# Three of eight up projections as seven products, and short products ahead of the down projections

## The chip, the cores and the metric

The kernel runs on one core of a Trainium2 chip. The metric is device time in microseconds (us). The kernel before takes 867.45 us (median of 3 runs, 867.34 to 867.73). A separate, profiled execution gave the page and the trace; the profile's rows are read from that one execution.

## What the kernel computes

One decoder layer on 512 tokens of width 1024, all in float32:

```python
h = rmsnorm(x)
q, k, v, xr, gr, g_attn, g_rnn = split(h @ w_in)          # seven blocks of 1024 columns
A = differential attention(q, k, v)                        # 8 heads, QK-norm, relative bias, causal
R = gelu(gr) * rg_lru(causal_conv4(xr))
x = x + (sigmoid(g_attn) * (A @ w_proj_attn) + sigmoid(g_rnn) * (R @ w_proj_rnn)) @ w_out
h2 = rmsnorm(x)
x = x + square(relu(h2 @ w_up)) @ w_down                   # 1024 -> 4096 -> 1024
```

The change touches the last two lines above all, and what runs beside the recurrent branch R.

## The kernel before

**Split float32.** A product of float32 operands is made of three passes in a rounded format. Each operand is split into a high part (a cast, on ACT) and a rest (source minus high part, a subtraction on DVE). `mm3` adds high x high, high x rest and rest x high into one accumulator. So every weight tile of 128 x 1024 (512 KB) costs one load, one cast on ACT and one subtraction on DVE: `wraw` or `raw` is the loaded tile, `whi` the cast and `wlo` the rest. There are five pairs of `whi` and `wlo` in the MLP, so weights are prepared up to four ahead, and four buffers for loads (`wraw` x2, `rx` x2).

**Stages.** Tokens lie along the columns of the moving operand. In order: the projections of `w_in` (q, k and v with attention mixed in, lines 136 to 138, products of 256 columns with `hT` as the stationary operand), the gates and the recurrent branch (products of 512 columns), the merge with `w_proj_*`, then `w_out` (`merged`), then the MLP. V tiles (`v`) and probability tiles (`pt`) are the operands of attention times V.

**Weights up to `w_out`.** Two objects of the class `Weights`, `wa` and `wb`, hold two streams of weight tiles that share two load buffers. In the recurrent part each has one load outstanding (`raws` = 1): the next load starts when the rest of the tile before it has been made. `wb` brings the 16 tiles of the recurrent branch's own projections.

**The MLP** is written out as a list of `steps`. The width of 4096 is cut into eight up groups of 512 columns, and the down projection into four pairs: pair d reads up groups 2d and 2d+1 and makes both halves of the output, (d, 0) and (d, 1). The order before is: up 0, 1, 2, down pair 0, up 3, 4, down pair 1, up 5, 6, down pair 2, up 7, down pair 3.

**Plain up group:** 8 blocks of the width 1024, 4 blocks of 128 output columns, 3 passes: 96 matmuls of 512 columns. Its result goes through relu and square on ACT (`up_out`) into `q`.

**Down product:** each (d, m) is a 2 x 2 block product done as seven products (Strassen's scheme in Winograd's form, named M1 to M7) in place of eight. One product has 2 x 4 x 3 = 24 matmuls of 256 columns, so (d, m) has 168. For it the activations are kept in seven forms: the four blocks and three more made of their sums and differences (`fs`; there are four sums, `FORM` says which form a product reads). The weights are summed as well: M5 takes b0 + b1, M6 takes b0 + b1 + b3, M7 takes b1 + b3, M4 takes b2 plus the sum. These sums are made in SBUF, by DVE (`plus`) and by accumulating transfers of POOL's queue. An output is added up by DVE (`down_out`) as soon as its product is done.

**Order of the work.** ACT, DVE and POOL run in the order in which the program is written (`InOrder`). `ahead` casts the next weights after each step. `later(us, f)` puts a piece of work some us of PE time later in that order; `tick` moves this clock on.

Of the kernel before, what the change touches and what calls it, by code (L numbers as in the profile page):

```python
# [37 lines left out]
def tile_block(ctx: ExitStack, tc: tile.TileContext, x, w_in, w_rga, w_rgx, w_pa, w_pr, w_o,  # L38
# [7 lines left out]
    sm = ctx.enter_context(tc.tile_pool(name="sm", bufs=4))  # L46
    es_ps = ExitStack()
# [169 lines left out]
    hT = hp.tile([P, 2 * KT * S + 64], F32R, tag="hT", name="hT")  # L217
    hT = [hT[:, 16 + j * KT * S:16 + (j + 1) * KT * S].rearrange("p (k s) -> p k s", k=KT) for j in range(2)]
# [38 lines left out]
    for j in range(4):  # L257
        wb.cols(w_o, 256 * j)
# [119 lines left out]
    wk = es_at.enter_context(tc.tile_pool(name="wk", bufs=1, reuse_waits="tile"))  # L378
    toep = [wk.tile([P, S], F32, tag=f"toep{h}", name=f"toep{h}") for h in range(NH)]
# [37 lines left out]
    def lam_diff(lt):  # L417
        lv = lt[:, :256].rearrange("p (a b c) -> p a b c", a=2, b=2)
        pv = lt[:, 256:384].rearrange("p (a c) -> p a c", a=2)
        V.tensor_tensor(out=pv, in0=lv[:, :, 0, :], in1=lv[:, :, 1, :], op=ALU.mult)  # L420
        t2 = lambda n: sm.tile([P, 2], F32, name=n, tag=n, bufs=1)
        ls, le = t2("ls"), t2("le")
        V.tensor_reduce(out=ls, in_=pv, axis=AX.X, op=ALU.add)
        A.activation(le, ls, AF.Exp)
        V.scalar_tensor_tensor(out=lneg, in0=le[:, 1:2], scalar=-LAMBDA_INIT, in1=le[:, 0:1], op0=ALU.add, op1=ALU.subtract)

    def softplus():
        lam = smt[:, C_LM:C_LM + KT]
        t8 = lambda n: sm.tile([P, KT], F32, name=n, tag=n, bufs=1)
        ab, e, den, s, s2, po, tmp, mx = (t8(n) for n in ("ab", "e", "den", "s", "s2", "po", "tmp", "mxl"))  # L430
# [391 lines left out]
    with tc.tile_pool(name="rp", bufs=1, reuse_waits="tile") as rp:  # L822
        fill = chain(ga, y_attn())
        side = []

# [40 lines left out]
        mh = hp.tile([P, 2, KT, S], F32R, tag="hT", name="mT")  # L866
        mh = [mh[:, j] for j in range(2)]
# [6 lines left out]
    h2T = [fin.tile([P, KT, S], F32R, tag=f"h2T{j}", name=f"h2T{j}") for j in range(2)]  # L874
# [3 lines left out]
    onesr = fin.tile([P, P], F32R, name="onesr")  # L878
    r2 = fin.tile([P, S], F32, name="r2")
    scratch = fin.tile([P, 4, S], F32, tag="us1", name="scratch")  # L880
    V.memset(scratch[:, 0, :P], 1.0)
    V.tensor_copy(onesr, scratch[:, 0, :P])
    ssq = scratch[:, 1, :]
    owing = []

    def merged(j):
        def done(ps):
            for c in range(2):
                t = 2 * j + c
                V.tensor_tensor(out=x2[:, t, :], in0=ps[c], in1=x2[:, t, :], op=ALU.add)  # L890
                split(h2T[0][:, t, :], h2T[1][:, t, :], x2[:, t, :], smt[:, C_G2 + t:C_G2 + t + 1])
            for c in range(2):
                t = 2 * j + c
                sq = ssq if t == 0 else scratch[:, 2 + t % 2, :]
                A.activation(sq, x2[:, t, :], AF.Square)
                if t:
                    owing.append(lambda sq=sq: V.tensor_tensor(out=ssq, in0=ssq, in1=sq, op=ALU.add))
# [6 lines left out]
    for d, ups in enumerate(((0, 1, 2), (3, 4), (5, 6), (7,))):  # L904
        steps += [("up", 2 * n + i // 2, i % 2, None) for n in ups for i in range(4)]
        if d < 3:
            steps += [("dn", (d, m), p, every) for m in range(2) for p in ORDER7]
        else:
            g, r = range(3), range(3, 4)
            steps += [("dn", (d, 0), p, q) for q in (g, r) for p in ("M1", "M2", "M5")]  # L910
            steps += [("dn", (d, 0), p, every) for p in ("M6", "M7", "M3", "M4")]
            steps += [("dn", (d, 1), p, every) for p in ORDER7]
# [4 lines left out]
    for kind, a, p in ops:  # L917
        if kind == "up":
            loads.append(((kind, a, p), w_up[p, a]))
        else:  # L920
            b = w_dn[2 * a[0] + a[1]].rearrange("a b p c -> (a b) p c")
            for q in (0, 1, 3, 2):
# [22 lines left out]
    def can_cast():  # L945
# [5 lines left out]
        return all((kind, a, q) in raw for q in ((p,) if kind == "up" else uses[p]))  # L951
# [14 lines left out]
    def cast_hi():  # L966
# [4 lines left out]
        src = raw[kind, a, p if kind == "up" else uses[p][0]]  # L971
        own = n % 5 == 4
        hi, lo = weight_pair(0 if own else 64, fin if own else None)
# [4 lines left out]
    def cast_lo():  # L978
# [3 lines left out]
        if kind == "up":  # L982
# [10 lines left out]
        if not half:  # L993
            plus(len(units))
# [28 lines left out]
    forms = [None] * 8  # L1023

    def hi_part(dst, src):
        A.copy(dst[:, 0], src)

    def lo_part(dst, src):
        V.tensor_tensor(out=dst[:, 1], in0=src, in1=dst[:, 0].bitcast(F32), op=ALU.subtract)

    def up_out(a, ps):
        n = a // 2
        if a % 2 == 0:
            t = hp.tile([P, 7168], F32R, tag="hT", name="us") if n % 3 == 0 else fin.tile([P, 7168 + 64], F32R, tag=f"us{n % 3}", name="us")
            t = t if n % 3 == 0 else t[:, 48:48 + 7168]
            forms[n] = t.rearrange("p (r f h s) -> p r f h s", r=2, f=7, h=2)
        d = forms[n][:, :, :, a % 2, :]
        q = fin.tile([P, 2, 2, 256], F32, tag="q", name="q")
        fs = fin.tile([P, 4, 256], F32, tag="fs", name="fs")
        w = 0.0 if a == 15 else 1.0  # L1040
        for c in range(2):
            A.activation(q[:, c, ::-1, :], two(ps[c]), AF.Relu)
            A.activation(q[:, c], q[:, c], AF.Square)
        a11, a21, a22, a12 = q[:, 0, 1], q[:, 0, 0], q[:, 1, 0], q[:, 1, 1]

        def sums():
            for m, (x, y, op) in enumerate(((a21, a22, ALU.subtract), (fs[:, 0], a11, ALU.subtract), (a11, a21, ALU.subtract), (a12, fs[:, 1], ALU.add))):
                V.tensor_tensor(out=fs[:, m], in0=x, in1=y, op=op)

        def first_hi():  # L1050
            hi_part(d[:, :, 0], a11)
            hi_part(d[:, :, 1:3], q[:, 1])

        def first_lo():
            lo_part(d[:, :, 0], a11)
            lo_part(d[:, :, 1:3], q[:, 1])

        later(w * 1.0, first_hi)
        if w == 0:
            later(0.0, first_lo)  # L1060
        later(w * 2.5, sums)
        later(w * 3.5, lambda: hi_part(d[:, :, 3:7], fs))
        if w:
            later(3.6, first_lo)
        later(w * 5.0, lambda: lo_part(d[:, :, 3:7], fs))
# [18 lines left out]

    def norm2():
        s2 = fin.tile([P, 2, S], F32R, tag="us2", name="s2")
        split(s2[:, 0], s2[:, 1], ssq)
        ps = psum("acc")
        T.matmul(ps, onesr, s2[:, 0], start=True, stop=False)
        T.matmul(ps, onesr, s2[:, 1], start=False, stop=True)  # L1090
        V.tensor_scalar(out=r2, in0=ps, scalar1=1.0 / DM, scalar2=EPS, op0=ALU.mult, op1=ALU.add)
        for t in range(KT):
            later(2.0 + 2.5 * t, lambda t=t: V.tensor_tensor(out=x2[:, t, :], in0=x2[:, t, :], in1=r2, op=ALU.mult))
        later(32.0, lambda: V.reciprocal(r2, r2))

    for j in range(4):
        if j == 2:
            wb.raws = 2
        for n, _ in enumerate(merged(j)):
            load()  # L1100
            while owing and n == 1:
                owing.pop(0)()
            if j == 3 and len(wb.units) == len(wb.reqs):
                ahead()
    while owing:
        owing.pop(0)()
    slots[0] += 1
    seen, banks, ps = {}, {}, None
    for n, (kind, a, p, pairs) in enumerate(steps):
        o = kind, a, p  # L1110
        if kind == "dn" and a not in banks:
# [93 lines left out]
```

## Time and profile before

| | |
|---|---|
| median of 3 runs | 867.45 us |
| profiled execution | 867.03 us |
| its span, first to last instruction | 865.3 us |
| PE busy | 859.6 us, 5239 matmuls |
| DVE, ACT, POOL busy | 602.1, 427.1, 64.3 us |
| DMA | 99.28 MB |
| granted TensorE clock | 1.00 |

PE is TensorE's matmul row and PEld its weight loads, which overlap with it. DVE is VectorE, ACT ScalarE, POOL GpSimd, SP the engine that issues most loads. Rows of groups read "line engine operation out<-in shapes xcount | busy us, mean ns | idle time before". Matmuls are pipelined: a 256-column one lasts about 0.28 us, but the next starts after 0.11 to 0.12, so a pace is taken from starts and not from lengths. Stages in the trace: projections and attention up to about 287 us, recurrent part and merge 287 to 486, `w_out` 486 to 529, MLP from 529. Line 66 is the helper that issues everything on ACT, DVE and POOL.

### The profile page before, as it was taken

What the parts mean: (1) busy time and instruction counts of PE and PEld (TensorE: products, weight loads), DVE (VectorE), ACT (ScalarE), POOL (GpSimd) and SP (SyncE); (2) the same over time, 40 slices, a digit from 0 to 9 for tenths busy, and PEclk for the clock granted to TensorE, in tenths of its full rate; (3) what the DMA queues carried; (4) which work ended last, traced back from release to release, by engine and by line L of the source; (5) the groups of instructions that cost most, each with busy time, mean ns of one, the idle gap of its engine ahead of it and who ended that gap; (6) DMA issues with size and microseconds to landing.
All of it is one profiled execution on the core that took longest, in us unless ns stands there. A gap on an engine that the chain in (4) does not pass through costs nothing.

```text
span 865.3 us, 13211 instructions
## 1 busy us (share of the span) xinstructions
PE 859.6 (99%) x5239; PEld 756.8 (87%) x5239; DVE 602.1 (70%) x1052; ACT 427.1 (49%) x679; POOL 64.3 (7%) x71
## 2 busy tenths in 40 slices
PE   9999999999999999999999999999999999999998
PEld 7899999999888888888888888889988998899898
DVE  6765688887866345978876656777746775667577
ACT  7444356464545337577653335556345444544341
POOL 0031212213011100000000000000000000000000
PEclk9999999999999999999999999999999999999999
DMA  6358212221321443323213723223652364246354
GB/s 199 120 167 242 93 57 81 64 84 63 108 64 42 114 137 98 110 86 97 73 55 123 259 99 129 92 89 81 168 173 73 103 173 140 72 128 189 87 134 122
DMA packets 33118, 99.28 MB, mean 115 GB/s; under 512 B 3984, under 2 KB 8792, under 8 KB 33056
## 3 DMA queue, kind: packets, MB, share of 16 engines
q1 hardware_dynamic: 29856, 87.93, 31.2%
q0 software_dynamic: 3200, 10.50, 6.4%
q8 instruction: 41, 0.67, 0.3%
q14 instruction: 21, 0.17, 0.1%
HBM read 87.89 MB, written 4.76 MB: 107 GB/s over the span
## 4 chain that ended last, share of the span: by engine, by line
PE 93%; DVE 4%; ACT 2%; DMA 1%; issue 1%; SPq 0%
PE acc L136 22%; PE acc L137 22%; PE acc L138 22%; PE acc L1154 18%; PE at L532 2%; PE at L137 2%; PE at L136 2%; PE at L138 2%; PE at L566 1%; DVE wlo L66 1%; DVE pe L66 1%; PE at L484 1%; PE at L597 1%; ACT pe L66 1%; DMA xT<-in_x_dram 1%
## 5 line engine op out<-in xcount | busy, mean ns | idle before, releaser
L1154 PE MATMUL acc<-us,whi 128*128 128x256 f32 x896 | 157.7, 280 | 0.0
L66 DVE TENSOR_TENSOR wlo<-wraw,whi 128x1024 fp32r<-128x1024 f32 (+2 forms) x86 | 96.8, 1147 | 72.6 <-ACT whi L66 72.2
L66 ACT CAST whi<-raw 128x1024 fp32r<-128x1024 f32 x88 | 90.6, 1049 | 102.0 <-DVE raw L66 41.6
L1154 PEld LDWEIGHTS acc<-us,whi 128*128 128x128 f32 x896 | 136.8, 188 | 0.4
L1154 PE MATMUL acc<-us,wlo 128*128 128x256 f32 x448 | 125.5, 280 | 0.0
L66 DVE TENSOR_TENSOR wlo<-raw,whi 128x1024 fp32r<-128x1024 f32 x88 | 106.5, 1217 | 16.1 <-ACT whi L66 15.8
L136 PE MATMUL acc<-whi,hT 128*128 128x256 f32 x384 | 109.7, 286 | 0.0
L137 PE MATMUL acc<-wlo,hT 128*128 128x256 f32 x384 | 107.2, 279 | 0.2 <-DVE wlo L66 0.2
L138 PE MATMUL acc<-whi,hT 128*128 128x256 f32 x384 | 107.0, 279 | 0.0
L66 ACT CAST whi<-wraw 128x1024 fp32r<-128x1024 f32 (+2 forms) x86 | 82.5, 981 | 42.7 <-DMA wraw<-in_w_in_dram 29.0
L138 PE MATMUL acc<-h2T,wlo 128*128 128x512 f32 x256 | 99.6, 389 | 0.0
L136 PE MATMUL acc<-h2T,whi 128*128 128x512 f32 x256 | 99.6, 389 | 0.0
L137 PE MATMUL acc<-h2T,whi 128*128 128x512 f32 x256 | 99.6, 389 | 0.0
L1154 PEld LDWEIGHTS acc<-us,wlo 128*128 128x128 f32 x448 | 85.7, 191 | 0.0
L136 PE MATMUL acc<-hT,whi 128*128 128x512 f32 x208 | 82.2, 395 | 0.0
L137 PE MATMUL acc<-hT,whi 128*128 128x512 f32 x208 | 81.2, 390 | 0.0
L138 PE MATMUL acc<-hT,wlo 128*128 128x512 f32 x208 | 81.0, 389 | 0.0
L136 PEld LDWEIGHTS acc<-whi,hT 128*128 128x128 f32 x384 | 72.3, 188 | 4.3 <-issue 3.0
L137 PEld LDWEIGHTS acc<-wlo,hT 128*128 128x128 f32 x384 | 72.2, 188 | 1.0 <-issue 0.5
L138 PEld LDWEIGHTS acc<-whi,hT 128*128 128x128 f32 x384 | 72.2, 188 | 0.6 <-issue 0.4
L66 ACT ACTIVATE pe<-pe,nm 128x128 f32<-128x128 f32 (+3 forms) x64 | 35.5, 556 | 66.0 <-DVE nm L66 66.0
L66 DVE TENSOR_TENSOR x<-acc,x 128x512 f32<-128x512 f32 (+1 forms) x52 | 33.2, 646 | 40.4 <-PE acc L1154 31.0
(192 smaller groups left out, 1605.9 us busy)
## 6 DMA issues: line engine op xcount, KB each, us to landing
wraw<-in_w_in_dram SPq DMA_DIRECT2D x54, 512.0 KB, 3.5
raw<-in_w_up_dram SPq DMA_DIRECT2D x32, 512.0 KB, 4.4
raw<-in_w_dn_dram SPq DMA_DIRECT2D x32, 512.0 KB, 3.5
raw<-raw POOLq DMA_DIRECT2D x16, 512.0 KB, 4.6
wraw<-in_w_pa_dram SPq DMA_DIRECT2D x8, 512.0 KB, 4.2
wraw<-in_w_pr_dram SPq DMA_DIRECT2D x8, 512.0 KB, 3.4
wraw<-in_w_o_dram SPq DMA_DIRECT2D x8, 512.0 KB, 3.5
trep<-tdram SPq DMA_DIRECT2D x8, 320.0 KB, 4.8
```

What stands on the lines that cost most here:

```text
L66: ins = f(*a, **k)
L136: T.matmul(o, l[0], r[0], start=first, stop=False)
L137: T.matmul(o, l[0], r[1], start=False, stop=False)
L138: T.matmul(o, l[1], r[0], start=False, stop=last)
L484: T.transpose(out=ps[:, t * P:(t + 1) * P], in_=qn[t // 2][:, c0:c0 + P], identity=ident)
L532: T.matmul(lg[c][:, :N], qT[r, x0, i * P:(i + 1) * P], kT[r, y0, :N], start=a == 0, stop=a == 2)
L566: T.transpose(out=tp[:, b * P:(b + 1) * P], in_=st[s][:, b * P:(b + 1) * P], identity=ident)
L597: T.matmul(ps[:, t:t + 1], sq[:, t * P:(t + 1) * P], ones, start=True, stop=True)
L1154: T.matmul(d, l[:, i, P * u:P * u + P], act[:, r, f, i % 2], start=p in ("M1", "M2", "M5") and k == z == e == 0 and (u == 0 or isinstance( ...
```

## The change

Up groups 2, 4 and 6 are done as seven products like the down projection; the other five stay plain. The order becomes, for d = 0 to 3: up 2d, up 2d+1, down pair d. For the seven products the moving operand `h2` holds the four blocks of each pair of width blocks and their four sums (made in `merged` for all), and the outputs are put together by `up_out` from the accumulators: M1 is copied out, M2 added, M5, M7, M6 and M3 combined, then relu and square. The summed weights (M5, M6, M7, M4 of three groups) are made by `weight_sums` with 30 transfers on POOL's queue, called at the head of the recurrent part: a tile is loaded, others are added to it on the way by accumulating loads, and each sum is stored in DRAM. There the groups load them like any weight.

A first product of 64 columns is put ahead of M1 of each (d, 0): it uses M1's first weights, and M1 starts its accumulator anew over it, so nothing of it stays ("empty"). `hT` and `mT` are cut into 14 slices and 2 (`Halves`; the last two live in the tile `tail`, which later holds sums). Ten small tiles move from the pool `sm` to the head of the attention pool, and fillers (`apart`, `apart2`) are added, so that V, the probability tiles and what follows stand at other addresses. Shifts of weight tiles change (`w_o` 64 bytes, plain up groups 0 or 192 in place of 64 or 0). The matmuls of the MLP are issued in written order too. The three-quarter first products of the last pair go.

```diff
+    stg = es_act.enter_context(tc.tile_pool(name="stg", bufs=1, side="right"))
+    summed = [{p: dp.tile([P, 1024], F32, name=f"up{n}{p}") for p in ("M5", "M7", "M6", "M4")} for n in range(2, 8, 2)]
+    def weight_sums():
+        t = stg.tile([P, 1024], F32, name="sum")
+        for n in range(2, 8, 2):
+            for blocks in (((0, None), (1, "M5"), (3, "M6"), (2, "M4")), ((1, None), (3, "M7"))):
+                for b, p in blocks:
+                    if p:
+                        G.dma_start(t, w_up[n, b], accum_op=ALU.add)
+                        G.dma_start(summed[n // 2 - 1][p], t)
+                    else:
+                        G.dma_start(t, w_up[n, b])
...
     wk = es_at.enter_context(tc.tile_pool(name="wk", bufs=1, reuse_waits="tile"))
+    t2 = {n: wk.tile([P, 2], F32, name=n) for n in ("ls", "le")}
+    t8 = [wk.tile([P, KT], F32, name=n) for n in ("ab", "e", "den", "s", "s2", "po", "tmp", "mxl")]
+    wk.tile([P, 32], F32, name="apart2")
...
         side = []
+        weight_sums()
...
-                split(h2T[0][:, t, :], h2T[1][:, t, :], x2[:, t, :], smt[:, C_G2 + t:C_G2 + t + 1])
+                A.activation(q[:, 2 * c:2 * c + 2], x2[:, t, :].rearrange("p (u s) -> p u s", u=2), AF.Copy, scale=smt[:, C_G2 + t:C_G2 + t + 1])
+            for c in range(2):
+                hi_part(d[:, :, 2 * c:2 * c + 2], q[:, 2 * c:2 * c + 2])
+                lo_part(d[:, :, 2 * c:2 * c + 2], q[:, 2 * c:2 * c + 2])
+            def sums():
+                fs = fin.tile([P, 4, 256], F32, tag="fs", name="fs")
+                sums_to(fs, *(q[:, m] for m in (1, 0, 3, 2)))
+                hi_part(d[:, :, 4:8], fs)
+                late.append(lambda: lo_part(d[:, :, 4:8], fs))
...
+    for d in range(4):
+        if d:
+            products("up", 2 * d)
         else:
+            products("pl", 0, ("b0", "b2", "b1", "b3"))
+        products("pl", 2 * d + 1, ("b0", "b2", "b1", "b3"))
+        products("dn", (d, 0))
+        products("dn", (d, 1))
...
+    def up_out(n, p, X, Y, Z):
+        if p == "M1":
+            begin(n)
+            snap = fin.tile([P, 2, 256], F32, tag="fs", name="snap")
+            A.copy(snap, two(Y))
+            quads[n] = fin.tile([P, 4, 2, 256], F32, tag="q", name="q"), snap
+            return
+        q, snap = quads[n]
+        if p == "M5":
+            A.copy(q[:, 2], two(Z))
+        elif p == "M6":
+            A.copy(q[:, 3], two(Y))
+        elif p == "M2":
+            V.tensor_tensor(out=q[:, 1], in0=two(X), in1=snap, op=ALU.add)
+            later(1.0, lambda: squared(q, 1, 2))
...
+        elif p == "M7":
+            V.tensor_tensor(out=q[:, 2], in0=q[:, 2], in1=two(Y), op=ALU.subtract)
+        elif p == "M3":
+            V.tensor_tensor(out=q[:, 3], in0=two(Z), in1=q[:, 3], op=ALU.subtract)
+            later(1.0, lambda: squared(q, 2, 4))
...
+        elif p == "M4":
+            squared(q, 0, 1, two(Y))
+            fs = rests()
+            later(2.0, lambda: total(n, fs, 0, 1))
+            later(4.9, lambda: total(n, fs, 2, 3))
...
+    def plain_out(n, c, u, ps):
...
+        A.activation(q[:, 2 * c:2 * c + 2][:, ::-1, u], two(ps), AF.Relu)
+        A.activation(q[:, 2 * c:2 * c + 2, u], q[:, 2 * c:2 * c + 2, u], AF.Square)
...
+        for m in range(2):
+            total(n, fs, m, u=u)
+            part(n, hi_part, 3 + m, 4 + m, fs[0][:, m:m + 1, u], u)()
+        for m in range(2):
+            part(n, lo_part, 3 + m, 4 + m, fs[0][:, m:m + 1, u], u)()
...
+        if kind == "dn" and a[1] == 0 and p == "M1" and k == 0:
+            I.matmul((b[0] if isinstance(b, tuple) else b)[:, :64], hi[:, 0, :P], forms[2 * a[0]][:, 0, f, 0, :64], start=True, stop=True)
         for u in range(2):
             d = b[u][:, :256] if isinstance(b, tuple) else b[:, 256 * u:256 * u + 256]
             for z, i in enumerate(pairs):
                 for e, (l, r) in enumerate(((hi, 0), (hi, 1), (lo, 0))):
-                    T.matmul(d, l[:, i, P * u:P * u + P], act[:, r, f, i % 2],
+                    act = h2[:, r, i, ACT8[p]] if kind == "up" else forms[2 * a[0] + i // 2][:, r, f, i % 2]
+                    I.matmul(d, l[:, i, P * u:P * u + P], act, start=p in ("M1", "M2", "M5") and k == z == e == 0 and (u == 0 or isinstance(b, tuple)),
```

More of the change, by code (lines that the diff above doesn't have):

```diff
@@ L46, in tile_block @@
     sm = ctx.enter_context(tc.tile_pool(name="sm", bufs=4))
+    sm.tile([P, 16], F32, name="apart", bufs=1)
     es_ps = ExitStack()
@@ L865, in tile_block @@
         wb.ahead, wb.raws = 3, 2
-        mh = hp.tile([P, 2, KT, S], F32R, tag="hT", name="mT")
-        mh = [mh[:, j] for j in range(2)]
+        mh = Halves("mT", 16)
         run(y_rnn(mh))
@@ L950, in can_cast @@
         kind, a, p = ops[n]
-        return all((kind, a, q) in raw for q in ((p,) if kind == "up" else uses[p]))
+        return all((kind, a, q) in raw for q in (uses[p] if kind == "dn" else (p,)))
     added, cast = set(), set()
@@ L992, in cast_lo @@
             G.dma_start(raw[kind, a, "b1"], raw[kind, a, "b3"], accum_op=ALU.add)
-        if not half:
+        if not half and more:
             plus(len(units))
@@ L1022, in tile_block @@
     two = lambda b: b.rearrange("p (u s) -> p u s", u=2)
[L1023 to L1065, printed above, removed]
@@ new lines, in total, with rests @@
+    def total(n, fs, *ms, u=slice(0, 2)):
+        q = quads[n][0][:, :, u]
+        fs = [f[:, :, u] for f in fs]
+        for m in ms:
+            x, y, op = ((q[:, 0], q[:, 2], ALU.subtract), (fs[0][:, 0], q[:, 1], ALU.subtract), (q[:, 1], q[:, 0], ALU.subtract), (q[:, 3], fs[0][:, 1], ALU.add))[m]
+            V.tensor_tensor(out=fs[m // 2][:, m % 2], in0=x, in1=y, op=op)
+    def rests():
+        return hp.tile([P, 2, 2, 256], F32, tag="tail", name="fs"), fin.tile([P, 2, 2, 256], F32, tag="fs", name="fs")
```

229 lines of the change are left out of this document (155 added, 74 removed).

## The prediction

> **What bounds the kernel now.** I read the page first (busy shares, the chain of waits), then the chain by stretches, then the TensorE rows whose first and last start give a pace, then the rows of the weight path (DMA, cast, rest) where PE comes nearest to waiting.
>
> ```profile
> span 865.3 us, 13211 instructions
> PE 859.6 (99%) x5239; PEld 756.8 (87%) x5239; DVE 602.1 (70%) x1052; ACT 427.1 (49%) x679; POOL 64.3 (7%) x71
> ...
> PE 93%; DVE 4%; ACT 2%; DMA 1%; issue 1%; SPq 0%
> ```
>
> The chain that ended last runs 93% through PE, at full granted clock. So the sum is one of matmul counts times paces, plus whatever new waits the change makes. The paces, from the view of one tile (plain up stage, products of 512 columns), from the chain (down stage, products of 256; columns: start, length, what; the first pair, the last one, its end) and from the groups of the page:
>
> ```profile
> L138 PE MATMUL acc<-h2T,wlo x69: 389/389/393, 548.7 to 595.0; 128*128 128x512 f32 x69
> 595.38 39.57 PE acc L1154 x336
> 822.90 38.83 PE acc L1154 x336
> 836.90 24.83 PE acc L1154 x219
> L1154 PE MATMUL acc<-us,whi 128*128 128x256 f32 x896 | 157.7, 280 | 0.0
> ```
>
> In the up stage every third matmul is one of these 69, so a 512-column matmul takes (595.0 - 548.7) / (68 x 3) = 0.2270 us. A 256-column one takes 39.57 / 336 = 0.1178 us in the first of the four down pairs, and the two in the middle are as long ((157.7 - 38.83) / 3 = 39.6); but in the end of the last pair it takes 24.83 / 219 = 0.1134 us. These are two paces of the same products, 0.0044 us apart. I call them slow and fast. Where they change (timeline of PE: start, length, what; a row may hold several):
>
> ```profile
> 190.12 0.28 PE L138 MATMUL acc<-whi,hT 128*128 128x256 f32 x1
> 190.82 0.28 PE L138 MATMUL acc<-whi,hT 128*128 128x256 f32 x1
> ...
> 222.91 0.60 PE L484 MATMUL at<-ident,qn 128*128 128x128 f32 x4
> 223.26 0.37 PE L136 MATMUL acc<-whi,hT 128*128 128x256 f32 x1
> 223.47 0.28 PE L137 MATMUL acc<-wlo,hT 128*128 128x256 f32 x1
> 223.58 0.28 PE L138 MATMUL acc<-whi,hT 128*128 128x256 f32 x1
> ...
> 834.28 0.36 PE L1154 MATMUL acc<-us,wlo 128*128 128x256 f32 x1
> 834.48 0.40 PE L1154 MATMUL acc<-us,whi 128*128 128x256 f32 x2
> ```
>
> At 834.28 one product starts 0.20 us before the next instead of 0.12, and from 836.90 at the latest the pace is the fast one and stays so. At 222.91 four short transposes come between; the stream after them settles at 0.113 too. At 190.12, a few matmuls behind another batch of short ones, the pace is 0.117 (six starts in 0.70 us): that one settled slow. So a hiccup of PE can switch the pace, in most cases to fast. A stream that follows 512-column products without one is slow from its first matmul: all four down pairs start that way.
>
> **The change part by part.** The sum is made against the profiled execution (865.3 us, 867.0 with what lies around it); the median shown is 867.45, 0.4 above, and I carry differences over to that.
>
> *Up groups 2, 4, 6 as seven products.* Each loses 96 matmuls of 512 columns and gains 7 x 24 = 168 of 256. Removed: 288 x 0.2270 = 65.4 us. Added: 504 x 0.1134 = 57.1 at the fast pace, 504 x 0.1178 = 59.4 at the slow one. Term: **-8.2** (slow: -6.0). By the rows a 256-column product costs half a 512-column one. The Trainium skill (TensorE: Matmul & The Clock Gate, Back-to-back issue gap) says otherwise: sustained 131 ns for 512 columns and 81 for 128. An estimate on a straight line gives 98 for 256, and by it three groups would cost 3 x (168 x 98 - 96 x 131) ns = 11.7 us more instead. This case's 227 and 113 to 118 ns disagree, and the measurement decides.
>
> *Empty products at the head of four down pairs.* Each is one 64-column matmul with the first weights between the 512-column stream and the down products; this is the place where slow begins now. If it acts like the short matmuls at 222.91, all 1344 down products and the seven-product group that follows each pair run fast. The four pairs take 3 x 39.57 + 38.83 = 157.5; 1344 x 0.1134 = 152.4. Term: **-5.2** (slow throughout: +0.8, since the last pair loses its fast part). One empty product costs between 0.11 (one weight load, as two fast products are apart) and 0.25 (a break such as 223.26 to 223.47, with settling): four cost **+0.6**.
>
> *V elsewhere.* Ten small tiles move from one pool to the head of the attention pool, so V and the probability tiles get other addresses.
>
> ```profile
> L138 PE MATMUL at<-pt,v x48: 276/281/283, 103.9 to 283.5; 128*128 128x256 f32 x48
> L136 PE MATMUL acc<-whi,hT x384: 276/276/390, 41.2 to 225.7; 128*128 128x256 f32 x192
> L1154 PE MATMUL acc<-us,whi x145: 276/276/276, 836.9 to 861.3; 128*128 128x256 f32 x145
> ```
>
> The triples are shortest, median and longest in ns. A fast product lasts 276 (last row), so attention-times-V is mostly slow (median 281) and the projections, which come after breaks as well, are mostly fast. 144 products, between 144 x 0.0044 = -0.6 and 0; I take **-0.3**. The same for hT, whose last two slices move: nothing, with the same kind of unknown.
>
> *Sums of weights in the recurrent part.* 30 transfers of 512 KB on POOL's queue, one after the other through one staging tile (6 loads, 12 accumulating loads, 12 stores). Between this row and its first add of the down stage POOL has nothing,
>
> ```profile
> 291.07 0.54 POOL L66 DMA_DIRECT2D rb<-rdram  x1 [1.71 <-ACT gate L66]
> wraw<-in_w_in_dram SPq DMA_DIRECT2D x54, 512.0 KB, 3.5
> raw<-in_w_up_dram SPq DMA_DIRECT2D x32, 512.0 KB, 4.4
> raw<-raw POOLq DMA_DIRECT2D x16, 512.0 KB, 4.6
> ```
>
> so they start at 292 and, at 4.6 us and an issue each, need some 150 to 165 us, until 450; the first down pair comes at 573, their first reader after 600. They are not late themselves, but they run beside the weight loads of the recurrent part, of which one is outstanding at a time there, exactly where PE has no reserve (ACT's casts with what they waited for, then the rests on DVE, then PE's first use of a rest):
>
> ```profile
> 305.31 2.00 ACT L66 CAST whi<-wraw 128x1024 fp32r<-128x1024 f32 x2 [3.02 <-DMA wraw<-in_w_in_dram]
> 311.29 1.05 ACT L66 CAST whi<-wraw 128x1024 fp32r<-128x1024 f32 x1 [3.98 <-DMA wraw<-in_w_in_dram]
> ...
> 306.40 2.36 DVE L66 TENSOR_TENSOR wlo<-wraw,whi 128x1024 fp32r<-128x1024 f32 x2 [3.32 <-ACT whi L66]
> 312.37 1.23 DVE L66 TENSOR_TENSOR wlo<-wraw,whi 128x1024 fp32r<-128x1024 f32 x1 [3.61 <-ACT whi L66]
> ...
> 307.94 0.39 PE L138 MATMUL acc<-hT,wlo 128*128 128x512 f32 x1
> 314.74 0.39 PE L138 MATMUL acc<-hT,wlo 128*128 128x512 f32 x1
> 337.86 0.39 PE L138 MATMUL acc<-hT,wlo 128*128 128x512 f32 x1
> ```
>
> The rest made first at 306.40 (half of 2.36, so ready at 307.6) is used at 307.94: 0.3 us to spare. The next, ready at 313.6, is used at 314.74: 1.1. Each cast waits for its load and each load for the rest before it, so d more per landing comes to 2d - 0.3 and 3d - 1.1 at these two. The chain turns round in 6.0 us (305.31 to 311.29), PE takes a unit every (337.86 - 307.94) / 4 = 7.5, so with d under 1.5 it catches up again. For d I take what up loads land later than the lone ones, 4.4 - 3.5 = 0.9 (they lie beside POOL's adds and each other): 3 x 0.9 - 1.1 = **+1.6**. Ends: 0 with d under 0.2; 7.0 with the longest landing that the up and down loads show below (6.2, d = 2.7) for these two alone.
>
> *Loads, casts and outputs in the seven-product groups.*
>
> ```profile
> DMA to landing us min/median/max: 3.3/4.4/6.2
> L66 ACT CAST whi<-raw x88: 1034/1049/1057, 522.4 to 852.1; 128x1024 fp32r<-128x1024 f32 x88
> L66 DVE TENSOR_TENSOR wlo<-raw,whi x88: 1161/1217/1227, 523.5 to 853.2; 128x1024 fp32r<-128x1024 f32 x88
> L66 ACT ACTIVATE q<-acc 128x512 f32<-128x512 f32 x11 | 6.5, 591 | 22.4 <-PE acc L138 22.4
> 595.00:635.00 40.00, 40.00 (x339) 39.94 (x338) 29.48 (x36) 18.26 (x22) 1.71 (x2) 1.00 0.61 168
> ```
>
> Seven loads in place of four: 7 x 0.52 MB in 19 us is 193 GB/s, a little over the 168 of the down pair at 595. By these rows (1.05 and 1.22 us for 1024 elements, 0.59 for 512 on ACT; what is half as wide on DVE costs a little over half, I take 0.69) ACT gets 7 casts (7.3), three copies of accumulators (1.8), relu and square (about 4.6) and four high parts (3.8): 17.5 us of the group's 168 x 0.1134 = 19.05. DVE gets 7 rests (8.5), three combinations (2.1), four sums (2.8) and four rests of outputs (4.3): 17.7. Both fit, barely. The last 8 us of it fall into the plain group behind, which needs some 13 of its 21.8 us on each; weights are cast four units ahead (11 us). Cover gone, each us over 19.05 would cost PE one: 0 to +3 for three groups.
>
> *Handing over.* Plain group to down pair: the last outputs go through relu, square, one difference, high part and rest. With 0.39 for the last matmul, 0.6 for 512 elements and 0.4 for 256, that is 0.39 + 0.6 + 0.6 + 0.4 + 0.4 + 0.4 = 2.8 us. They are wanted after the first product and nine matmuls of the second, (24 + 9) x 0.1134 = 3.74: 0.9 to spare, at each of the four pairs. Merge to first up group: sum, scaled copies, high part and rest end about 3.0 us after the last w_out product, wanted after 18 x 0.227 = 4.1. The four extra blocks of differences there lie beside 11 us of PE each. For this paragraph and the one above together I take **+0.5**, between 0 and 5.
>
> At nothing: the norm's two matmuls, which only come later; the other order of the down blocks, since their casts run ahead as before; and nine more loads on SP's queue, which issues in 0.33 us and is idle between loads. Without that cover each would show as a late cast, priced above.
>
> Sum: -8.2 - 5.2 + 0.6 - 0.3 + 1.6 + 0.5 = **-11.0**, so 867.45 - 11.0 = 856.5 us.
>
> **The rivals.** *The empty product does not switch the pace.* The stream at 190.12 stayed slow after its break. With all slow: -6.0 + 0.8 + 0.4 + 0 + 1.6 + 0.5 = -2.7, 864.7 us; half of the places slow: 860.6. For it: two settled outcomes of similar breaks exist. Against: the projections' median of 276 says that most settle fast.
>
> *The sums of weights starve the recurrent part* (the one that ends slower). From d = 1.5 on, the one-load chain is slower than PE, and each of some 13 further units of the recurrent part that go through it (16 units of the two recurrent projections) loses d - 1.5. Without its +1.6 the sum is -12.6. At d = 2.3 (landing 5.8): 3 x 2.3 - 1.1 + 13 x 0.8 = 16 us, and 867.45 - 12.6 + 16 = 871; at d = 2.7, 7.0 + 15.6: 877. It decides from a landing of 5.7 on, where the loss passes 14.3. For it: 6.2 was seen. Against: the median beside other transfers is 4.4, and POOL has one transfer in flight.
>
> *Half a product costs more than half.* Above 65.4 / 504 = 0.130 us a matmul the seven products gain nothing, about 867 with the down pairs as they are. The slowest steady row is 0.1178. It would make the change come out at 0 or worse. The Trainium skill's figures above would be this case.
>
> **How the numbers follow.** Forecast 0.52; pace partly or all slow 0.27; starved 0.10; half a product dearer 0.02; ACT or DVE late in the seven-product groups or at the handings-over, by 5 to 10 us, 0.09 (862 to 867). Low end: -8.2 - 5.2 + 0.4 - 0.6 = -13.6, so 853.9. High end: the slow case, 865. Measurement tells 0.2% (1.7 us) from no change: faster (under 865.7) is the forecast, nearly all of the slow case and half of the late one, 0.83; slower 0.10; the rest, 0.07, the same.
>
> **What would show it.** In the chain, the four down pairs as 1344 products at 0.1134 and the seven-product groups at 19.05 us each; a 0.1178 there is the first rival. PE starts late by 1 to 2 us between 301 and 340, with ACT's casts waiting longer for the loads; more than 10 us is the second. POOL's queue done near 450. Wrong outright I would be if PE waited in the seven-product groups for casts or accumulators, or if a 256-column product with the new operands took over 0.12.

## The result, and the profile after

The changed kernel takes 858.44 us (median of 4 runs, 857.36 to 861.0) against 867.59 for the kernel before on the same chip: a ratio of 0.9899, 95% interval 0.9876 to 0.9921, so 9.2 us or 1.1% faster. On a second chip, once more: 859.37 against 868.28, ratio 0.9902 (0.9884 to 0.9920). The profiled execution below is the quickest of the first four, 857.36 us.

The page of the changed kernel (lines are one higher than before; what the MLP issues on PE now shows as line 67, since it goes through the helper of written order):

```profile
span 855.6 us, 13733 instructions
PE 848.4 (99%) x5459; PEld 755.4 (88%) x5459; DVE 627.6 (73%) x1069; ACT 449.2 (52%) x703; POOL 84.7 (10%) x101
```

PE still fills 99% of the span: 220 matmuls more, and 11.2 us less of busy time. Where the MLP begins, the view of one tile tells (its first and last start stand behind the shortest, median and longest duration), of the kernel before and then of the changed one; where it ends, the changed kernel's chain from 570 us on (start, length, what):

```profile
L136 PE MATMUL acc<-h2T,whi x256: 388/389/398, 529.2 to 822.1; 128*128 128x512 f32 x128
```

```profile
L67 PE MATMUL acc<-h,whi x656: 276/276/398, 532.1 to 812.8; 128*128 128x256 f32 x84, 128*128 128x512 f32 x80
```

```profile
569.98 281.64 PE acc L67 x2168
```

The MLP starts at 532.1 instead of 529.2, 2.9 us later. Its products end at 569.98 + 281.64 = 851.6; before, by the last pair of the chain, at 822.90 + 38.83 = 861.7. So the MLP gained 13.0 us, and the part ahead of it lost 2.9. The rest of the text is about these two numbers. (What follows the last product takes 0.4 longer, which makes the 9.7 between the two spans.)

**The MLP.** Stretches of it, a seven-product group three times, a plain group and a down pair (columns: stretch, length, then busy time and instructions of PE, PEld, DVE, ACT and POOL, granted clock, DMA share, GB/s):

```profile
614.40:633.45 19.05, 19.05 (x171) 19.05 (x170) 15.33 (x14) 11.21 (x15) 0.00 (x0) 1.00 0.60 198
693.45:712.50 19.05, 19.05 (x170) 19.05 (x170) 12.25 (x13) 11.17 (x14) 0.00 (x0) 1.00 0.61 206
772.50:791.50 19.00, 19.00 (x170) 19.00 (x169) 12.22 (x13) 11.15 (x14) 0.00 (x0) 1.00 0.62 195
633.45:655.20 21.75, 21.75 (x99) 17.99 (x98) 15.45 (x18) 14.14 (x20) 0.86 (x1) 1.00 0.35 97
576.20:614.40 38.20, 38.20 (x339) 38.20 (x338) 31.39 (x40) 18.27 (x22) 2.60 (x3) 1.00 0.59 164
```

A group as seven products takes 19.05 us for 168 products, 0.1134 each; a plain one 21.8. The down pair takes 38.2 where it took 39.57. PE has no gap in any of them, and ACT and DVE, which were to be nearly full in the seven-product groups, are busy 11.2 and 12 to 15 of 19.05 us.

How the pace starts (timeline of PE; the first row of `us` holds the empty product and the first two products):

```profile
576.17 0.51 PE L67 MATMUL acc<-us,whi 128*128 128x64 f32 x3
576.51 0.28 PE L67 MATMUL acc<-us,wlo 128*128 128x256 f32 x1
576.63 0.39 PE L67 MATMUL acc<-us,whi 128*128 128x256 f32 x2
576.85 0.28 PE L67 MATMUL acc<-us,wlo 128*128 128x256 f32 x1
```

From 576.17 to 576.51 the empty product and two full ones go by; from then on three products take 0.34 us, 0.113 each, at once. Two products would have taken 0.227 of the 0.34, so an empty one costs 0.11 us, as much as a full one with four times its columns: a break lies behind it.

**The part ahead of the MLP.** Late starts of PE in the recurrent part, with what released them, and ACT's casts there:

```profile
300.32 0.39 PE L139 MATMUL acc<-hT,wlo 128*128 128x512 f32 x1
301.03 0.50 PE L137 MATMUL acc<-hT,whi 128*128 128x512 f32 x1 [0.32 <-ACT gate L67]
301.37 0.40 PE L138 MATMUL acc<-hT,whi 128*128 128x512 f32 x1
301.99 0.50 PE L139 MATMUL acc<-hT,wlo 128*128 128x512 f32 x1 [0.23 <-DVE wlo L67]
...
308.98 0.50 PE L137 MATMUL acc<-hT,whi 128*128 128x512 f32 x1 [0.35 <-ACT whi L67]
...
310.24 0.50 PE L139 MATMUL acc<-hT,wlo 128*128 128x512 f32 x1 [0.52 <-DVE wlo L67]
```

```profile
298.49 2.00 ACT L67 CAST whi<-wraw 128x1024 fp32r<-128x1024 f32 x2 [7.09 <-DMA wraw<-in_w_pa_dram]
300.39 1.07 ACT L67 ACTIVATE gate<-acc 128x512 f32<-128x512 f32 x2
...
307.88 1.99 ACT L67 CAST whi<-wraw 128x1024 fp32r<-128x1024 f32 x2 [4.13 <-DMA wraw<-in_w_in_dram]
```

PE should start every 0.227 us. From 300.32 to 301.03 it is 0.71, so 0.48 late; likewise 0.40 at 301.99, 0.51 at 308.98 and 0.70 at 310.24, and the start after each is 0.11 late as well. That makes 2.5 us. Behind it stands ACT. Of its casts in the kernel before, the first at this place is

```profile
297.01 2.00 ACT L66 CAST whi<-wraw 128x1024 fp32r<-128x1024 f32 x2 [5.47 <-DMA wraw<-in_w_pa_dram]
```

It is now at 298.49 and has waited 7.09 for its load in place of 5.47; the one at 305.31 is at 307.88. The first of these loads wasn't issued later (SP's queue, before and then changed; each row holds two issues, and its start is that of the first):

```profile
292.82 6.85 SPq L100 DMA_DIRECT2D wraw<-in_w_pa_dram  x2
```

```profile
292.69 8.47 SPq L101 DMA_DIRECT2D wraw<-in_w_pa_dram  x2
```

So it is the transfer that takes longer: the cast comes 5.8 us behind the issue in place of 4.2. The gate at 300.39 had to wait behind the first of these casts, since ACT works in written order. The loads (median us from issue to landing) and the traffic between 300 and 330 us (of the kernel before, then of the changed one):

```profile
wraw<-in_w_in_dram SPq DMA_DIRECT2D x54, 512.0 KB, 3.9
...
sum<-in_w_up_dram POOLq DMA_DIRECT2D x18, 512.0 KB, 5.5
...
wraw<-in_w_pa_dram SPq DMA_DIRECT2D x8, 512.0 KB, 5.5
```

```profile
300.00:330.00 30.00, 30.00 (x134) 24.84 (x133) 15.29 (x18) 10.44 (x13) 0.00 (x0) 1.00 0.44 141
```

```profile
300.00:330.00 30.00, 28.58 (x123) 22.38 (x122) 14.38 (x17) 10.07 (x14) 3.41 (x5) 1.00 0.76 211
```

The DMA engines are busy 0.76 of the time instead of 0.44. `w_in` tiles land 0.4 us later in the median (3.5 before), those of the attention's output projection 1.3 later (4.2 before).

### The profile page after: what moved, and what is told of

The parts are those of the page before. It is cut to its first block, busy times and chain, and to the rows that moved or that the text cites. A ratio compares the mean times of both kernels' runs of the same rounds, so it can differ in the third digit from the quotient of the medians.

```text
span 855.6 us, 13733 instructions
## 1 busy us (share of the span) xinstructions
PE 848.4 (99%) x5459; PEld 755.4 (88%) x5459; DVE 627.6 (73%) x1069; ACT 449.2 (52%) x703; POOL 84.7 (10%) x101
## 4 chain that ended last, share of the span: by engine, by line
PE 93%; DVE 3%; DMA 1%; ACT 1%; SPq 0%; issue 0%; DVEq 0%
PE acc L67 37%; PE acc L137 15%; PE acc L139 15%; PE acc L138 15%; PE at L563 2%; PE at L139 2%; PE at L137 2%; PE at L138 2%; DMA wraw<-in_w_in_dram 1%; DVE wlo L67 1%; PE at L597 1%; PE at L515 1%; PE at L628 1%; ACT whi L67 1%; DVE pe L67 1%; ACT pe L67 1%
## 5 line engine op out<-in xcount | busy, mean ns | idle before, releaser
L67 PE MATMUL acc<-h,whi 128*128 128x512 f32 (+1 forms) x656 | 155.7, 331 | 0.0
L67 PE MATMUL acc<-us,whi 128*128 128x256 f32 (+1 forms) x900 | 153.0, 276 | 0.0
L67 DVE TENSOR_TENSOR wlo<-raw,whi 128x1024 fp32r<-128x1024 f32 x97 | 117.5, 1218 | 14.0 <-ACT whi L67 13.8
L67 PEld LDWEIGHTS acc<-h,whi 128*128 128x128 f32 x656 | 110.5, 188 | 12.3
L137 PE MATMUL acc<-whi,hT 128*128 128x256 f32 x384 | 109.8, 286 | 0.0
L67 PE MATMUL acc<-h,wlo 128*128 128x256 f32 (+1 forms) x328 | 108.6, 331 | 0.0
L137 PE MATMUL acc<-hT,whi 128*128 128x512 f32 x208 | 82.5, 396 | 0.7 <-ACT whi L67 0.3
L139 PE MATMUL acc<-whi,hT 128*128 128x256 f32 x288 | 80.4, 279 | 0.0
L137 PEld LDWEIGHTS acc<-whi,hT 128*128 128x128 f32 x384 | 72.4, 188 | 4.3 <-issue 3.0
L67 PEld LDWEIGHTS acc<-h,wlo 128*128 128x128 f32 x328 | 61.6, 188 | 6.3
L138 PE MATMUL acc<-hT,whi 128*128 128x512 f32 x156 | 60.9, 391 | 0.0
L67 POOL TENSOR_TENSOR rs<-ms,mhalf 128x8 f32<-128x8 f32 (+1 forms) x25 | 39.7, 1589 | 206.7 <-DVE ms L67 206.7
```

Source lines behind the costliest of these rows:

```text
L67: ins = f(*a, **k)
L137: T.matmul(o, l[0], r[0], start=first, stop=False)
L138: T.matmul(o, l[0], r[1], start=False, stop=False)
L139: T.matmul(o, l[1], r[0], start=False, stop=last)
```

## The experiments

All times are medians beside runs of the kernel before on the same chip; "changed" is the kernel after.

**Without the sums.** `weight_sums()` isn't called, and the groups load plain blocks of `w_up` in place of the sums.

```diff
         side = []
-        weight_sums()
...
-            loads.append(((kind, a, p), w_up[a, int(uses[p][0][1])] if p in ("M1", "M2", "M3") else summed[a // 2 - 1][p]))
+            loads.append(((kind, a, p), w_up[a, int(uses[p][0][1])]))
```

> Leaves the sums of weights out: no transfer of POOL's queue in the recurrent part, and the seven-product groups load a plain block in place of each sum, so their output is not that of the layer; every load, cast and product of the MLP stays. Theory (the 30 transfers make weight loads land late): PE has no late start between 300 and 312 us, 855 us, 2 to 5 below the changed kernel, spread under 1 us. Rival (the late starts come from the moved tiles or the order): the late starts stay and the time with them, 857 to 861.

**The sums later.** Nothing is left out; they begin when the second recurrent projection is under way (about 329 us). The `memset` by DVE, whose order is written, is what holds POOL's queue back until then: the first load into the tile has to wait for it. It was run on two chips.

```diff
     def weight_sums():
         t = stg.tile([P, 1024], F32, name="sum")
+        V.memset(t[:, :8], 0.0)
...
-        weight_sums()
...
+            if j == 1:
+                weight_sums()
```

> The same 30 transfers, but the first waits for a small write on DVE at the second quarter of the recurrent part (about 330 us), past the first units, where the weights of before had 0.3 and 1.1 us to spare. Theory (it hurts only where nothing is to spare): late starts under 1 us in sum, 855 to 856.5 us, spread under 1.5. Rival (any place in the recurrent part costs the same): 857.5 or more, late starts between 340 and 460 us of 2 us or more.

> The kernel with late sums once more, beside the split one on one chip: 857 us, 10 to 11 us under the kernel before, no start of TensorE late by more than 0.1 us between 300 and 345 us.

**The changed kernel again**, beside the first two:

> The changed kernel as it is, timed again beside the next three. Its four runs lie between 857.4 and 861.0 us, those of the kernel before within 0.6. If the loads that land late in the recurrent part decide (theory), the spread stays: median 857.5 to 860, runs 2 to 4 us apart, and PE starts late at the first units after 300 us, by 2 to 6 us in sum. If the spread was an accident of one chip, the runs lie within 1 us.

| kernel | us | ratio to before, 95% |
|---|---|---|
| changed, second chip | 859.37 | 0.9902 (0.9884 to 0.9920) |
| no sums, second chip | 855.21 | 0.9854 (0.9839 to 0.9868) |
| late sums, second chip | 857.05 | 0.9873 (0.9858 to 0.9888) |
| late sums, another chip | 856.38 | 0.9869 (0.9855 to 0.9884) |

So the sums cost 859.37 - 855.21 = 4.2 us on that chip, and moving them by 37 us wins 2.3 back. The median of late sums there is a little over the 855 to 856.5 that was expected, but under the rival's 857.5, and the place matters as the theory had it. The same stretch with late sums:

```profile
300.00:330.00 30.00, 30.00 (x134) 24.84 (x134) 16.04 (x20) 10.55 (x14) 0.53 (x1) 1.00 0.42 136
```

The DMA share is back at 0.42, and PE at 134 matmuls in the 30 us, as in the kernel before; without sums both numbers are the same. That the sums at this place make PE late is shown; that it is by their traffic is argued from the longer landings and the fuller DMA engines. The profile of the changed kernel's second set (860.99 us, the slowest of that set) shows more than late starts (stretches, then PE's timeline):

```profile
301.00:312.00 11.00, 8.66 (x35) 5.92 (x34) 4.96 (x6) 4.06 (x6) 1.19 (x2) 1.00 0.68 201
312.00:316.20 4.20, 4.20 (x12) 3.29 (x13) 0.95 (x1) 0.00 (x0) 0.22 (x1) 0.59 0.76 170
```

```profile
313.64 0.63 PE L138 MATMUL acc<-hT,whi 128*128 128x512 f32 x1
314.07 0.63 PE L139 MATMUL acc<-hT,wlo 128*128 128x512 f32 x1
```

Here the late starts between 301 and 312 come to 3.4 us, and then the granted clock falls to 0.59 for 4.2 us: products start 0.427 us apart instead of 0.227, which costs another 1.6.

**The sums split, and the sums apart.** What late sums still lose against no sums is at 433 us and at 600, in some executions. Two more placements: group 6 held back until about 470 us (split, the diff), and groups 4 and 6 (apart, with `(2,)` and `(4, 6)` in its place).

```diff
-    def weight_sums():
-        t = stg.tile([P, 1024], F32, name="sum")
-        for n in range(2, 8, 2):
+    def weight_sums(ns):
+        t = stg.tile([P, 1024], F32, name="sum", tag="sum")
+        V.memset(t[:, :8], 0.0)
+        for n in ns:
...
+            if j == 1:
+                weight_sums((2, 4))
...
-        run(y_rnn(mh))
+        for n, _ in enumerate(y_rnn(mh)):
+            if n == 13:
+                weight_sums((6,))
```

> The sums of groups 2 and 4 begin, as in the kernel with late sums, once the second recurrent projection is under way; those of group 6 begin only at about 456 us, behind the places at 432 and 440 us where that kernel's TensorE still lost about 0.1 us. If contention for the loads is all that the sums cost, nothing is left to gain but those 0.1 us and the noise of loads that land late: 0 to 1 us less than late sums, 856 to 857 us. If sums that run beside w_out and the first up group collide with the loads there (0.14 us of lost time is seen at 591 us with late sums), it is slower than late sums by up to 2 us.

> Only the sums of group 2 run beside the recurrent projections, from about 328 to 380 us; those of groups 4 and 6 begin behind the last recurrent work on ACT, at about 470 us, and end near 570. In the kernel with split sums a cast at 420 us waited 5.8 us for its load, 2.8 more than without sums, ACT's work behind it moved by 2.3 us, and TensorE waited 1.6 us at 433 for it. If that wait belongs to the sums running at that time, it goes, no start of TensorE between 290 and 460 us is more than 0.15 us late, and the time is 855 to 856.5 us, as without sums. If the loads of w_out and of the first up groups suffer instead, late starts appear between 486 and 614 us and the time stays at 857 to 858.

Split: 857.59 us, ratio 0.9881 (0.9864 to 0.9897), no better than late sums. It is not the loads of `w_out` that lose, as the slower case of the expectation had it: the sums of group 4 still run at 420 us, and there they hit ACT. Its row without sums, and with split ones (each with the row that PE waits for):

```profile
418.26 2.00 ACT L67 CAST whi<-wraw 128x1024 fp32r<-128x1024 f32 x2 [3.03 <-DMA wraw<-in_w_pr_dram]
...
429.72 1.27 ACT L67 ACTIVATE tt<-at,hb 128x512 f32<-128x512 f32 x2
```

```profile
420.61 2.00 ACT L67 CAST whi<-wraw 128x1024 fp32r<-128x1024 f32 x2 [5.84 <-DMA wraw<-in_w_pr_dram]
...
432.08 1.27 ACT L67 ACTIVATE tt<-at,hb 128x512 f32<-128x512 f32 x2
```

One cast waits 2.8 us longer for its load, everything that ACT does behind it moves by 2.35, and PE, which wants `tt`, starts 1.6 us late at 432.82.

Apart: 883.92 us, ratio 1.0185 (1.0171 to 1.0199), far outside both expectations. Starts of PE before 486 us are clean, as expected, but (waits by engine, then DVE's timeline):

```profile
PE acc L67 <- DVE s L67: 26.0, 1, 26.0
```

```profile
539.20 0.42 DVE L67 TENSOR_TENSOR fs<-q,fs 128x256 f32<-128x256 f32 x1
573.70 1.23 DVE L67 TENSOR_TENSOR wlo<-raw,whi 128x1024 fp32r<-128x1024 f32 x1 [34.08 <-DMA up6M<-sum]
```

```profile
578.40:581.60 3.20, 3.20 (x9) 2.49 (x8) 3.17 (x4) 1.97 (x2) 0.00 (x0) 0.54 0.67 219
```

DVE stands still from 539.6 to 573.7, until the last sum has been stored out of the staging tile. The rest that it then writes, `wlo`, is the first of the fifth pair, which lies in the pool `fin`; `fin` is opened after the pool of the staging tile is closed, and takes its memory. Behind it in DVE's order comes `s`, the operand of the norm's matmuls. PE waits 26 us for `s`, and then runs 3 us at a granted clock of 0.54. So the sums have an earlier end date than their first reader: 540 us, when their tile's memory is written anew.

**Without empty products, and the empty products alone.** The first takes the four away from the changed kernel, the second puts them into the kernel before (the same line in its function of the down products).

```diff
-        if kind == "dn" and a[1] == 0 and p == "M1" and k == 0:
-            I.matmul((b[0] if isinstance(b, tuple) else b)[:, :64], hi[:, 0, :P], forms[2 * a[0]][:, 0, f, 0, :64], start=True, stop=True)
```

> The changed kernel without the four 64-column products; nothing else differs. Theory (they switch the pace): all down pairs at 0.1178 us a product, 39.6 us in place of 38.1, and the three seven-product groups at 19.8 in place of 19.05: 4 x 1.5 + 3 x 0.74 = 8.1 us more, less 0.5 for the products themselves: 866 us. Rival (the order of the groups or the addresses made the pace fast): no change, 858.

> The kernel before, with nothing added but the four 64-column products ahead of the down pairs. Theory (a short product switches the pace by itself): all 1344 down products at 0.1134 us, 152.5 us in place of 157.5, less 4 x 0.12 for the added ones: 4.5 us faster than the kernel before. Rival (the switch needs the new order or the new addresses): pairs at 39.6 us, and 0.5 us slower.

865.84 us, ratio 0.9984 (0.9970 to 0.9998), and 863.40, ratio 0.9952 (0.9935 to 0.9968). The chain without them (to be read against 281.64 us for 2168 products above), and the first pair's products (shortest, median, longest in ns):

```profile
569.84 289.37 PE acc L67 x2164
```

```profile
L67 PE MATMUL acc<-us,whi x221: 280/281/281, 576.0 to 614.9; 128*128 128x256 f32 x111
```

All four pairs and all three seven-product groups run slow then: 7.7 us for 1848 products, 0.0042 each. In the kernel before, with them, the first pair (the two behind it are as long) and the tail of the fourth:

```profile
596.15 38.19 PE acc L1156 x336
...
829.78 1.14 DVE wlo L66
830.97 27.49 PE acc L1156 x238
```

39.57 has become 38.19 in each. The last pair gained nothing (39.0 us from its first product to its end in both kernels), since most of it was fast before, and since it now comes upon a rest that DVE makes only at 829.78 (PE starts 0.27 us late at 830.97): 3.8 us in all, not 4.5.

**How short must it be, and how often?** 256 or 128 columns in place of 64; and 64 at the first pair only.

```diff
-            I.matmul((b[0] if isinstance(b, tuple) else b)[:, :64], hi[:, 0, :P], forms[2 * a[0]][:, 0, f, 0, :64], start=True, stop=True)
+            I.matmul((b[0] if isinstance(b, tuple) else b)[:, :256], hi[:, 0, :P], forms[2 * a[0]][:, 0, f, 0, :256], start=True, stop=True)
...
-        if kind == "dn" and a[1] == 0 and p == "M1" and k == 0:
+        if kind == "dn" and a == (0, 0) and p == "M1" and k == 0:
```

> The changed kernel, with 256 columns in place of 64 in the four empty products, so that no product in the stream is short. Theory (a short product is what switches: the weight load behind it is exposed once): down pairs and seven-product groups stay slow, 39.6 and 19.8 us, 866 as without them. Rival (any product there does it, since the same weights are loaded twice in a row or the accumulator starts anew): fast pace, 38.1 and 19.05 us, and 858 to 859.

> The first product ahead of each down pair has 128 columns, between the 64 that switched the pace and the 256 that did not. If any product whose weight load is not covered by a full 256-column product before it switches, then all four pairs run at 0.113 us, 858 to 860 us. If it takes a product as short as 64 columns, the pairs run at 0.118 and it ends at 865 to 866 us.

> The changed kernel, with the empty product at the first down pair alone. Theory (512-column products set the pace back to slow, and a 256-column stream keeps the pace that it has): first pair and the seven-product group behind it fast, 38.1 and 19.05 us; the three other pairs 39.6 and the two other groups 19.8. Three pairs x 1.5 + two groups x 0.74 = 6.0 us over the changed kernel. Rival (once switched, the fast pace lasts): all fast, no more than the changed kernel.

256 columns: 865.95 us, ratio 0.9992 (0.9983 to 1.0001), as if there were none. 128 columns: 859.21, ratio 0.9917 (0.9889 to 0.9944), as with 64. The first pair with 256, then with 128:

```profile
L67 PE MATMUL acc<-us,whi x221: 280/281/282, 576.1 to 614.9; 128*128 128x256 f32 x111
```

```profile
L67 PE MATMUL acc<-us,whi x225: 223/276/368, 576.9 to 615.0; 128*128 128x256 f32 x112, 128*128 128x128 f32 x1
```

So it isn't one more product that does it, but a short one. I take the break behind it for the cause, since the short transposes in the prediction had one too; this is argued, not shown. With one empty product, at the first pair alone (864.13 us, one run), the second pair is slow from its first product:

```profile
L67 PE MATMUL acc<-us,whi x220: 280/281/282, 656.4 to 695.0; 128*128 128x256 f32 x110
```

But the first pair did not stay fast to its end:

```profile
600.08 0.28 PE L67 MATMUL acc<-us,wlo 128*128 128x256 f32 x1
...
600.42 0.28 PE L67 MATMUL acc<-us,wlo 128*128 128x256 f32 x1
600.57 0.47 PE L67 MATMUL acc<-us,whi 128*128 128x256 f32 x2
600.88 0.28 PE L67 MATMUL acc<-us,wlo 128*128 128x256 f32 x1
...
601.24 0.28 PE L67 MATMUL acc<-us,wlo 128*128 128x256 f32 x1
```

Up to 600.42 three products take 0.34 us; the three from 600.42 to 600.88 take 0.46, and the next three 0.36: a break has switched the stream back to slow. It stays slow, and the seven-product group behind the pair, which was expected fast, is slow too (a median length of 281 ns from 614.8 to 634.3). So the run does not show what the expectation said, that 512-column products undo the switch: the stream ahead of them was slow already, and no other run here settles it. What the runs show is that a 256-column stream behind 512-column products starts slow where no short product comes first.

**V elsewhere, alone.** The kernel before with the ten small tiles moved.

> The kernel before, with nothing changed but the ten small tiles and the fillers, so that V and the probability tiles stand where the change puts them. Theory: attention times V becomes fast in part, its 144 products gain at most 0.6 us; median length 281 ns goes to 276 if all of them switch. Rival (the pace there hangs on the break ahead and not on the address): median stays 281, under 0.2 us gained.

867.21 us in one run, against 867.24 of the kernel before on that chip. Attention times V there, the last of its three passes:

```profile
L139 PE MATMUL at<-pt,v x48: 276/281/286, 103.6 to 283.7; 128*128 128x256 f32 x48
```

Still a median of 281 ns, the slow pace, as before; in the changed kernel it is 281 as well.

## Why the prediction was right, and where it was off

The prediction, 856.5, was 1.9 us low. The terms below make 0.9 of it (-10.1 in place of -11.0). Another 0.4 is what follows the last product, where the prediction had nothing, and the rest comes from setting a profile against medians: the median lies 1.1 us over the profiled execution of the changed kernel and 0.4 over that of the kernel before. Term by term, in the profiled executions (the products end at 851.6 instead of 861.7: -10.1):

| term | predicted | measured | from |
|---|---|---|---|
| groups as seven products | -8.2 | -8.3 | 19.05 + 19.05 + 19.00 against 65.4 |
| down pairs, empty products included | -5.2 + 0.6 | -4.7 | 4 x 38.2 against 157.5 |
| V elsewhere | -0.3 | 0 | median 281 ns in all three kernels |
| sums in the recurrent part | +1.6 | +2.9 | MLP starts at 532.1, not 529.2 |
| handing over, ACT and DVE in the groups | +0.5 | 0 | no gap of PE |

*Half a product costs half a product.* Right, to 0.1 us; the rival that it costs more than 0.130 us fell with the first row.

*The empty product switches the pace.* Right at all four places, and the most valuable single line of the change: without it, 865.84. What the prediction knew of it was an inference from short transposes; that shortness is the point, the runs with 256 and 128 columns show. Without the switch the prediction's own rival gave 864.7; the run without empty products came to 865.84 with sums that cost more than assumed, so the sizes agree as well. Its price was set at 0.11 to 0.25 each and is 0.11.

*Sums in the recurrent part.* The step that was mis-sized. The mechanism was as written (loads land later, ACT's casts and DVE's rests follow, PE waits, and it catches up), and so were the sign and the order: no starving, although the loads of the output projection landed at 5.5 us, close to the 5.7 from which that rival was to decide. But the reserve was taken from the casts of `w_in` at 305 and 311, and the delay d from the up loads in the median, 0.9. The load one place ahead, of the output projection, lands 1.3 us later; ACT's gate stands behind its cast, and PE was late at 301 already, by 1.1 us with the starts behind, and by 1.4 at 309 and 310. That is 2.5 of the 2.9; another 0.4 fell at 434 and 442, where the prediction had no term. By their casts the two loads came 1.5 and 1.1 us later, in place of 0.9 each, and with these the prediction's own 2d - 0.3 comes to 1.5 + 1.1 - 0.3 = 2.3, close to the 2.5: the chain was right, and the delay per load too small. And one thing it did not have at all: behind the late starts of one execution the clock fell, which cost 1.6 us there. Both may be why the changed kernel spreads more (857.4 to 861.0) than without sums (854.8 to 855.9); this is argued from two profiles.

*They are not late themselves.* True as it stands: the last sum is issued at 453 us. But the slack was read from the wrong date. First reader after 600 was the argument; the sums apart show that the staging tile has to be empty at 540.

*V elsewhere.* The value taken, -0.3, was wrong; the end 0 of its bounds is what both runs show. An address that was moved did nothing for the pace of that stream.

*Handing over.* The 0.9 us to spare at each pair held. In a seven-product group and the plain one behind it DVE is busy 15.33 + 15.45 = 30.8 us, ACT 25.4; the prediction's figures make 17.7 + 13 and 17.5 + 13. So DVE was counted well and ACT too high, and neither made PE wait.

The kernel with late sums is faster than the changed one: 856.4 to 857.1 us, ratio 0.987 on two chips.

What stays open: what in PE the two paces are. The runs show when a stream is fast or slow and what switches it, not what it is that differs. A break of 0.12 us switched it to slow (600.57 above), while one of 0.22 in the same run (at 592 us) and one of 0.5 at 600 us in the kernel with late sums left it fast; which way a break falls, no run here tells in advance.

## What to carry to other kernels

A stream of products may have two steady paces, 4% apart, and keep one until a break switches it; compare the starts at the head and the tail of long uniform stages, and where they differ, try one short product at the head. Work that an idle queue does "for free" costs what its traffic takes from the loads beside it, so put it where the loads have slack, and check the end date of the memory that it uses as well as that of its result. Where an engine works in written order, one late load delays everything written behind its cast: the reserve has to be taken at the first such place, not at the typical one.

## What the hardware showed that was not expected

The clock. In the second profile of the changed kernel no single stop of PE was over 1.3 us, yet after 3.4 us of late starts within 11 us the granted clock was 0.59 over the next 4.2. In the first profile, 2.5 us of late starts in the same place had no such effect. The Trainium skill (TensorE: Matmul & The Clock Gate, What's actually happening) has the clock fall to half after an idle window of about 3.4 us and come back after a busy one, which fits the 3 us at 0.54 behind the 26 us stop of the sums apart; the drop after short stops only is a case that this rule does not cover. The products under the lowered clock of the second profile start 0.427 us apart at 512 columns. The Trainium skill (TensorE: Matmul & The Clock Gate, Wait — 56ns, not 53.3ns?) gives 427 ns for the cold clock, and the trace agrees.

A break costs PE more than the wait: behind each of the four late starts between 301 and 311 us of the changed kernel the next one is late by 0.11 us as well (301.03 to 301.37 is 0.34 us for a product of 0.227).
